# Attention block: transposed probabilities meet the values two slots later, and two instructions get a fixed place in their engines' orders

## Chip, cores and metric

The kernel runs as one program on 1 core of one Trainium2 chip. The metric is device time in microseconds (us) of one execution, the median of several runs. Below, PE is the tensor engine (with PEld its weight loader), DVE the vector engine, ACT the scalar engine, POOL the GpSimd engine and SP the sync engine, which here issues nearly all transfers, in one fixed order.

## What is computed

One hybrid block on a sequence of 1024 tokens and 1024 channels: a convolution branch, an attention branch, a gated sum of both, and a feed-forward part. The change lies in the attention branch. Cut to it, the reference is

```python
for window, dilation in ((128, 1), (512, 4), (2048, 16)):
    o_g, lse_g = dilated_window_attention(q, k, v, slopes, window, dilation)   # blocks of 128, previous and own block as keys
    outs.append(o_g); lses.append(lse_g)
mix = softmax(stack(lses), axis=0)          # per token and head, over the three groups
o = einsum('gbsh,gbshd->bshd', mix, stack(outs))
y_b = o.reshape(B, S, ATTN_DIM) @ w_attn_out
```

There are 16 heads of 64 channels. Matrix products are made at more than one rounded product's accuracy: each operand is split into a rounded part and its remainder (`hi` and `lo`, `ph` and `pl`), and the products of the parts are summed.

## The kernel before

**Slots.** The attention stage is a software pipeline of 128 slots, 8 for each of the 16 heads, followed by 13 more in which it drains (loop at L1114 to L1172). PE, ACT, DVE and POOL run in the order in which this loop is written. SP is not in that list: a scheduler places its transfers, by their dependencies and by when it expects them to be ready. A slot `at` has the place `at % 8` in its head. In order, a slot does the following.

- `score` (L928 to L954): the products of queries and keys for one group of query blocks. Places 0 to 3 score blocks 3, 2, 1, 0 (the head's first half); place 4 scores `far` (queries of the second half against keys of the first, by residue mod 4); places 5, 6 and 7 score blocks 7, 6, and 4 with 5. DVE adds the mask and takes the row minimum (`least`, L928 in the profile), ACT exponentiates (`powers`, L972).
- `fill(FRONT[place])`: filler steps for PE. One step is three 128x512 matmuls of another product (gate logits, then the convolution's output projection, tiles `gate` and `ya`, L120 to L122), whose results are spilled.
- `flip` of the slot 12 earlier (`BACK`): PE transposes up to four 128x128 pieces of probabilities into the PSUM tile `pp` (L1023), ACT rounds it to `ph` (L1044), DVE takes the remainder `pl` (L1045). Places 4, 5 and 6 flip the groups (0), (1), (2,3) of the first half, place 7 nothing, places 0 to 3 the groups far, (4), (5), (6,7,3) of the second.
- `weigh` of the groups that the slot before flipped (list `pend`): PE multiplies `ph` (L1061) and `pl` (L1062) with the values `v` or `vf` into the PSUM tile `o`, one tile for each half head. After a half's last group, `result` (L1065) copies `o` to `ot` on ACT (L1070) and spills it.
- `fill(BEHIND[place])`: more filler steps.

`pp`, `o`, `gate` and `ya` share one pool of four PSUM banks (`psB`); a bank is given to the next tile when its last reader is done.

**Statistics of the second half.** Far and near scores of the same token must be normalised together, though they lie on different partitions. Each side therefore sends its row minimum and sum to the other's layout: `near_to_far` by four small transfers (L989, `other<-own`), `far_out` and `far_to_near` by a write to DRAM and a read of it (L992 `dstat<-own`, L995 `other<-dstat`). `far_out` belongs to place 6, `near_to_far` to place 0 and `far_to_near` to place 1 of the next head. At place 5 DVE compares the two (`compare`, L999), at place 6 `combine` (L1006 to L1008) forms the factors, and POOL scales the probabilities by them (`times`, L975), the far ones first. Then the flips of places 0 to 3 may run.

**Loads.** At place 1 `head(h + 1)` asks for the next head's queries, keys (two transfers `kk`) and mask (`m`, L749); at place 5 `values` asks for `v` and `vf`.

**Before the slots.** The last step of the stage ahead is a product into the PSUM tile `gx` (`product(X, ...)`, L878), which ACT copies away as `c` (L880). The pool of two large PSUM tiles that holds `gx` then holds score tiles.

Of the kernel before, what the change touches and what calls it, by code (L numbers as in the profile page):

```python
# [32 lines left out]

LAG = 2
WARM = 7
FRONT = (0, 2, 0, 1, 0, 1, 1, 0)
BEHIND = (0, 0, 0, 1, 2, 0, 1, 1)
BACK = 12
READ = 5
COPIES = (-1, 0, 1)  # L40
APART = (2, 3, 4, 5, 6)
START = (1, 1, 1, 1, 0, 0, 0, 0, 0, 0, 0, 0)
# [19 lines left out]
def block_kernel(ctx: ExitStack, tc: tile.TileContext, x, xT, x0, g2, pack, mask,  # L62
# [243 lines left out]
    if True:  # L306
# [426 lines left out]
        def conv_result(c):  # L733
# [4 lines left out]
                           scale=pk[:, C_CG + c : C_CG + c + 1])  # L738
            act.dma_start(da[:, c, :], ordered)

        def head(h):
            hp, r, g8 = h // 2, (h % 2) * DH, h // 8
            q = p2.tile([P, T], F32R, tag="q", bufs=2, name=f"q_{h}")
            kk = p2.tile([P, 2, T], F32R, tag="kk", bufs=2, name=f"kk_{h}")
            m = p2.tile([P, 640], F32, tag="m", bufs=2, name=f"m_{h}")
            fetch(q, dq[g8].rearrange("p s c t -> (p s) c t")[2 * r : 2 * r + P, hp % 4, :])
            for s in range(2):
                fetch(kk[s:P:2], dk[g8][r : r + DH, :, hp % 4, :])
            sp.dma_start(m, mask[h])  # L749
            return q, kk[:, 0], kk[:, 1], m  # L750

        cover(COVER)
# [65 lines left out]
        with tc.manual_schedule(engines=hand):  # L818
            for n in range(2):
                xz[n] = gate_first(n, firsts[n])  # L820
                begun(n)
            load(1, 0)
            for n, (a, b) in enumerate(PAIRS):
                X = xz[n][:, 0:512]
                Y = bank_ps(f"gy_{n}")
                (sh, sl), (gh, gl) = pw[n]["s12"], pw[n]["s3"]
                inner = 0 < n < N - 1
                if n + 2 < N:
                    load(n + 2, 0)
                if n == 3:  # L830
                    p1_cm.__exit__(None, None, None)
                    p2_cm = tc.tile_pool(name="ph2", bufs=1, reuse_waits="tile")
                    p2 = p2_cm.__enter__()
                    pool2.append(p2)
                if n + 1 < N:
                    load(n + 1, 1)
                if n == 3:
                    tiles[0] = head(0)
                parts(n, "s4", "s4")
                if n == 0:  # L840
                    fourth()
                if inner:
                    parts(n + 1, 0, "v")
                product(X, sh[:, 4:8], sl[:, 4:8], *form["t2"], False)
                c12 = quarter(f"c12_{n}")
                act.activation(c12, X, AF.Copy)
                product(Y, sh[:, 0:4], sl[:, 0:4], *form["t1"], True)
                p5 = quarter(f"p5_{n}")
                act.activation(p5, Y, AF.Copy)
                if n == N - 1:  # L850
                    act.activation(warm, mhalf[:, 0:7], AF.Exp)
                if n == 0:
                    rs8 = conv_factors()
                if n == 2:
                    for c in (2, 3, 4, 5):
                        conv_result(c)
                product(X, gh[:, 0:4], gl[:, 0:4], *b12, False)
                if n == 1:
                    conv_spread(rs8)
                tt_(p5, X, p5, add)  # L860
                sp.dma_start(dgate[b][:, 512:1024], p5)
                if n + 1 < N:
                    sums(n + 1)
                if inner:
                    xz[n + 1] = big_ps(f"gx_{n + 1}")
                    for i in range(2):
                        product(xz[n + 1][:, i * 512 : i * 512 + 512], *(t[:, 4 * i : 4 * i + 4] for t in pw[n + 1]["v"]),
                                *left[i], True)
                    parts(n + 1, 2, "s12")
                    begun(n + 1)  # L870
                    for c in {1: (0, 1), 2: (6, 7)}.get(n, ()):
                        conv_result(c)
                else:
                    product(Y, *pw[n]["s4"], *b22, False)
                    tt_(c12, Y, c12, add)
                    if n + 1 < N:
                        parts(n + 1, 2, "s12")
                product(X, gh[:, 4:8], gl[:, 4:8], *form["t4"], False)  # L878
                c21 = quarter(f"c21_{n}")
                act.activation(c21, X, AF.Copy)  # L880
                sp.dma_start(dgate[b][:, 0:512], c21)
                if inner:
                    product(Y, *pw[n]["s4"], *b22, False)
                if n + 1 < N:
                    parts(n + 1, 1, "s3")
                if inner:
                    tt_(c12, Y, c12, add)
                sp.dma_start(dgate[a][:, 512:1024], c12)
# [7 lines left out]
    if True:  # L896
# [89 lines left out]

        def near_to_far(h):
            for i in range(4):
                sp.dma_start(other[h][32 * i : 32 * i + 32, 1], own[h][:, 0, i])  # L989

        def far_out(h):
            sp.dma_start(dstat[h % 2], own[h][:, 1])  # L992

        def far_to_near(h):
            sp.dma_start(other[h][:, 0], dstat[h % 2].rearrange("(i a) r s -> (a r) i s", i=4))  # L995

        def compare(h):
            f = ready2("both", [P, 2, 4], F32, 2, f"both_{h}")
# [111 lines left out]
        with tc.manual_schedule(engines={ENG.Activation, ENG.DVE, ENG.PE, ENG.Pool}):  # L1110
            apart = lambda at: at % 8 in APART or not 0 <= at < len(slots)
            pend = []
            fill(1)
            for at in range(len(slots) + BACK + 1):  # L1114
                count[2] += 1
                cur = slots[at] if at < len(slots) else None
                front, behind = (FRONT[at % 8], BEHIND[at % 8] + (START[at] if at < BACK else 0)) if cur else TAIL
                new = []
                if cur is not None:
                    h, half, n = cur  # L1120
                    place = at % 8
                    if place == 4:
                        statistics(h)
                    if place == 5:
                        values(h)
                    if place == 1 and h + 1 < H:
                        tiles[h + 1] = head(h + 1)
                    new = score(h, tiles[h], SCORES[half][n])
                for unit in late:
                    share(*unit)  # L1130
                if len(pieces) > 2 and apart(at):
                    piece_high(2)
                fill(front)
                for n, soon in enumerate(COPIES):
                    if at == 0 and soon < 0 or cur is not None and (at - soon) % 8 == 0 and at - soon < len(slots):
                        by_residue((at - soon) // 8 if at else 0, n)
                flips = []
                if BACK <= at < len(slots) + BACK:
                    fh, fhalf, fn = slots[at - BACK]
                    if FLIPS[fhalf][fn]:  # L1140
                        flips.append(flip(fh, fhalf, FLIPS[fhalf][fn]))
                for w in pend:
                    done = weigh(*w) or done
                pend = flips
                late = []
                if done is not None:
                    result(*done)
                    done = None
                for ago, ready in ((BACK - 2, combine), (BACK - 3, compare)):
                    if 0 <= at - ago < len(slots) and slots[at - ago][1:] == (1, 0):  # L1150
                        ready(slots[at - ago][0])
                for unit in new:
                    powers(*unit)
                if cur is not None and half == 0:
                    late = new
                for ago, n0, send in ((2, 0, far_out), (1, 3, near_to_far), (READ, 0, far_to_near)):
                    if 0 <= at - ago < len(slots) and slots[at - ago][1:] == (1, n0):
                        send(slots[at - ago][0])
                if at == len(slots):
                    p2_cm.__exit__(None, None, None)  # L1160
                    hb2.append(ctx.enter_context(tc.tile_pool(name="hb2a", bufs=1, reuse_waits="tile")))
                    oT = [[hb2[0].tile([P, KT, 512], F32R, tag=f"hb{a}0", name=f"oT{a}0")] for a in range(2)]
                    heads = [o_fetch(0, k) for k in range(0, KT - 2, 2)]
                if at - len(slots) in (4, 5, 8, 9, 10, 11, 12):
                    o_step(heads)
                if at == len(slots) + BACK - 4:
                    heads.append(o_fetch(0, KT - 2))
                if apart(at):
                    piece_low()
                fill(behind)  # L1170
                if apart(at + 1):
                    piece_high(2)  # L1172
            for _ in gates:
# [627 lines left out]
```

## Time and profile before

| What | us |
|---|---|
| median of 3 runs (1698.5 to 1700.75) | 1699.01 |
| the profiled execution's own time | 1695.4 |
| its span, first to last instruction | 1693.6 |
| of the span: slots of the attention stage, about | 570 to 878 |

The profile describes one execution. A row of a group names the line, the engine, the operation, output and inputs, shape and count, then busy time, mean duration of one, and the idle time ahead of it with what ended it. A row of waits names who waited and for what, the total, how many times, and the longest. A row of the timeline has the start, the duration, and in brackets the engine's idle time before it. Matmuls overlap, so the distance between starts, not the duration of one, is what a matmul costs. PE is reported busy for 1681.4 of 1693.6 us.

### The profile page before, as it was taken

How to read it: one execution, taken by the hardware profiler on the slowest of the kernel's cores; microseconds unless marked ns; L12 is line 12 of the kernel's file. 1: busy time of each engine (PE TensorE's matmuls, PEld its weight loads, DVE VectorE, ACT ScalarE, POOL GpSimd, SP SyncE). 2: the span in 40 equal slices, each digit the busy share in tenths (PEclk: the TensorE clock that was granted, in tenths of full speed). 3: DMA queues.
4: the chain of work that ended last, by engine and by line, in shares of the span. 5: the costliest groups of instructions: out<-in, count | busy, mean ns of one | idle time of the engine just before them, and what ended most of it. 6: DMA issues, size and time to landing. Idle time of an engine off the chain costs nothing.

```text
span 1693.6 us, 22622 instructions
## 1 busy us (share of the span) xinstructions
PE 1681.4 (99%) x7939; PEld 1397.1 (82%) x7939; DVE 1303.1 (77%) x2114; ACT 787.9 (47%) x1351; POOL 224.3 (13%) x300
## 2 busy tenths in 40 slices
PE   9999999999999999999999999999999999999999
PEld 7888888888888888888888888888888888888887
DVE  6999999999876567767658654887777677789863
ACT  5411233233245478767646433544544455543431
POOL 0000132033000255555410000000000000000000
PEclk9999999999999999999999999999999999999999
DMA  9411145344555977886769594622222222499851
GB/s 375 153 50 50 50 137 162 125 137 137 175 178 195 320 226 238 261 243 201 221 214 333 187 335 147 227 99 76 75 90 85 87 75 87 145 366 322 287 172 50
DMA packets 187121, 300.24 MB, mean 177 GB/s; under 512 B 32256, under 2 KB 90240, under 8 KB 186496
## 3 DMA queue, kind: packets, MB, share of 16 engines
q1 hardware_dynamic: 185712, 294.48, 52.1%
q10 hardware_dynamic: 1296, 4.33, 0.6%
q8 instruction: 62, 1.02, 0.2%
q14 instruction: 51, 0.42, 0.1%
HBM read 214.74 MB, written 83.95 MB: 176 GB/s over the span
## 4 chain that ended last, share of the span: by engine, by line
PE 92%; DMA 3%; DVE 2%; ACT 1%; issue 1%; SPq 0%; POOL 0%; ACTq 0%; DVEq 0%
PE dx L1607 7%; PE xz L144 6%; PE xz L145 6%; PE xz L146 6%; PE dy L1607 5%; PE qkv L139 5%; PE qkv L137 5%; PE qkv L138 5%; PE y L145 2%; PE y L144 2%; PE y L146 2%; PE pp L1023 2%; PE wo L138 2%; PE wo L139 2%; PE wo L137 2%; PE o L1062 2%
## 5 line engine op out<-in xcount | busy, mean ns | idle before, releaser
L137 PE MATMUL qkv<-hi_qkv,hT 128*128 128x512 f32 x384 | 151.2, 395 | 0.0
L139 PE MATMUL qkv<-hi_qkv,hT 128*128 128x512 f32 x384 | 149.8, 391 | 0.0
L138 PE MATMUL qkv<-lo_qkv,hT 128*128 128x512 f32 x384 | 149.8, 391 | 0.0
L1510 DVE SCALAR_TENSOR_TENSOR u<-u,pk 128x1023 f32<-128x1023 f32 x88 | 112.1, 1275 | 1.2 <-ACT u L1508 0.9
L113 POOL TENSOR_TENSOR rs<-ss,mhalf 128x8 f32<-128x8 f32 x32 | 66.3, 2074 | 294.0 <-DVE ss L112 294.0
L1045 DVE TENSOR_TENSOR pl<-pp,ph 128x512 fp32r<-128x512 f32 (+1 forms) x95 | 58.7, 618 | 46.7 <-ACT ph L1044 46.5
L586 DVE SCALAR_TENSOR_TENSOR cacc<-csum,both,cacc 128x512 f32<-128x512 f32 x120 | 89.4, 745 | 0.3
L586 DVE SCALAR_TENSOR_TENSOR cacc<-apad,pk,cacc 128x512 f32<-128x512 f32 x120 | 88.2, 745 | 0.0
L89 DVE TENSOR_TENSOR lo_uv<-raw_uv,hi_uv 128x1024 fp32r<-128x1024 f32 x20 | 24.5, 1226 | 79.4 <-ACT hi_uv L88 79.4
L139 PEld LDWEIGHTS qkv<-hi_qkv,hT 128*128 128x128 f32 x384 | 72.1, 188 | 15.0
L586 DVE SCALAR_TENSOR_TENSOR codd<-apad,pk,codd 128x513 f32<-128x513 f32 x112 | 83.7, 748 | 0.7 <-ACT codd L579 0.7
L138 PEld LDWEIGHTS qkv<-lo_qkv,hT 128*128 128x128 f32 x384 | 72.2, 188 | 14.3
L137 PEld LDWEIGHTS qkv<-hi_qkv,hT 128*128 128x128 f32 x384 | 72.1, 188 | 14.2
L928 DVE CUSTOM_DVE_ANT_0 p<-s,m 128x512 f32<-128x512 f32 (+1 forms) x120 | 59.1, 502 | 17.2 <-POOL pf L975 6.3
L1044 ACT ACTIVATE ph<-pp 128x512 fp32r<-128x512 f32 (+1 forms) x95 | 51.5, 542 | 43.9 <-PE pp L1023 43.1
L144 PE MATMUL xz<-h2left,hi_uv 128*128 128x512 f32 x176 | 68.6, 390 | 0.0
L144 PE MATMUL xz<-blk_t,hi_s3g 128*128 128x512 f32 x176 | 68.6, 390 | 0.0
L146 PE MATMUL xz<-h2left,lo_uv 128*128 128x512 f32 x176 | 68.5, 389 | 0.0
L145 PE MATMUL xz<-h2left,hi_uv 128*128 128x512 f32 x176 | 68.5, 389 | 0.0
L145 PE MATMUL xz<-blk_t,hi_s3g 128*128 128x512 f32 x176 | 68.5, 389 | 0.0
L146 PE MATMUL xz<-blk_t,lo_s3g 128*128 128x512 f32 x176 | 68.5, 389 | 0.0
L1508 ACT ACTIVATE u<-u,pk 128x1024 f32<-128x1024 f32 x44 | 54.5, 1239 | 9.5 <-DVE u L1497 4.5
(479 smaller groups left out, 5056.5 us busy)
## 6 DMA issues: line engine op xcount, KB each, us to landing
wr<-w_down SPq DMA_DIRECT2D x45, 512.0 KB, 5.9
kk<-dk SPq DMA_DIRECT2D x32, 512.0 KB, 6.1
gr<-dff SPq DMA_DIRECT2D x62, 256.0 KB, 5.4
raw_qkv<-w_qkv SPq DMA_DIRECT2D x24, 512.0 KB, 4.9
dff<-u SPq DMA_DIRECT2D x22, 512.0 KB, 2.6
raw_uv<-w_up SPq DMA_DIRECT2D x21, 512.0 KB, 3.7
raw_ug<-w_up SPq DMA_DIRECT2D x20, 512.0 KB, 3.6
dv<-v SPq DMA_DIRECT2D x16, 512.0 KB, 2.8
```

Of the source, the lines that this page charges most:

```text
L113: pool.tensor_tensor(out=dst, in0=tmp, in1=mhalf[:, : tmp.shape[1]], op=ALU.pow)
L137: pe.matmul(ps, ah, hi[:, k % 2, :], start=(k == 0), stop=False)
L138: pe.matmul(ps, ah, lo[:, k % 2, :], start=False, stop=False)
L139: pe.matmul(ps, al, hi[:, k % 2, :], start=False, stop=(k == KT - 1))
L144: pe.matmul(o, wh[:, k, :], bh[:, k, :], start=(start and k == 0), stop=False, skip_group_check=not start)
L145: pe.matmul(o, wh[:, k, :], bl[:, k, :], start=False, stop=False, skip_group_check=not start)
L146: end = pe.matmul(o, wl[:, k, :], bh[:, k, :], start=False, stop=(k == 3), skip_group_check=not start)
L586: dve.scalar_tensor_tensor(out=out_, in0=src[:, i : i + size], scalar=w(i), in1=out_, op0=ALU.mult, op1=ALU.add)
L928: dve.tensor_tensor_reduce(out=pt, in0=s, in1=m, scale=-1.0, scalar=3e38, op0=ALU.add, op1=ALU.min, accum_out=nm)
L1045: dve.tensor_tensor(out=runs(pl[:, c]), in0=order(pp[:, c]), in1=runs(ph[:, c]).bitcast(F32), op=ALU.subtract)
L1510: dve.scalar_tensor_tensor(out=acc[:, d:], in0=src[:, : T - d], scalar=w(2 - d), in1=acc[:, d:], op0=ALU.mult, op1=ALU.add)
L1607: pe.matmul(banks[n][:, cols], a[:, c], b[:, d], start=(start and i == 0 and m == 0), stop=(stop and i == nf - 1 and m == 2), skip_group_c ...
```

## The change

Groups flipped in one slot are multiplied with the values two slots later (`DEEP`), and one slot later again from the fourth slot of the drain (`NEAR_END`). The filler steps are dealt out anew: 10 for 8 slots as before, now 3 of them ahead of the flip and 7 at the slot's end, where it was 5 and 5. The load of the values moves from place 5 to place 6. The read of the far statistics is tied behind the last transfer noted in `queued`, which is the next head's mask load, or the last `near_to_far` transfer where no head follows. The filler step at the end of slot 0 is tied behind the last matmul of the product ahead of the slots.

```diff
-FRONT = (0, 2, 0, 1, 0, 1, 1, 0)
-BEHIND = (0, 0, 0, 1, 2, 0, 1, 1)
+FRONT = (0, 1, 0, 0, 0, 0, 1, 1)
+BEHIND = (0, 1, 0, 2, 2, 0, 1, 1)
 BACK = 12
 READ = 5
+DEEP = 2
+NEAR_END = 4
+VALUES = 6
...
+        queued = []
+
         def head(h):
...
-            sp.dma_start(m, mask[h])
+            queued[:] = [sp.dma_start(m, mask[h])]
...
-                product(X, gh[:, 4:8], gl[:, 4:8], *form["t4"], False)
+                paired = product(X, gh[:, 4:8], gl[:, 4:8], *form["t4"], False)
...
         def near_to_far(h):
             for i in range(4):
-                sp.dma_start(other[h][32 * i : 32 * i + 32, 1], own[h][:, 0, i])
+                queued[:] = [sp.dma_start(other[h][32 * i : 32 * i + 32, 1], own[h][:, 0, i])]
...
         def far_to_near(h):
-            sp.dma_start(other[h][:, 0], dstat[h % 2].rearrange("(i a) r s -> (a r) i s", i=4))
+            with tc.issue_after(queued[0].ins):
+                sp.dma_start(other[h][:, 0], dstat[h % 2].rearrange("(i a) r s -> (a r) i s", i=4))
...
-                    if place == 5:
+                    if place == VALUES:
                         values(h)
...
-                for w in pend:
-                    done = weigh(*w) or done
-                pend = flips
+                pend.append(flips)
+                while len(pend) > (DEEP if at < len(slots) + NEAR_END else 1):
+                    for w in pend.pop(0):
+                        done = weigh(*w) or done
...
-                fill(behind)
+                with tc.issue_after(paired.ins) if not at else ExitStack():
+                    fill(behind)
```

`tc.issue_after(x)` sets an order of issue on x's engine and no wait for x's end.

The instructions are the same on every engine; PE, ACT and SP run them in another order, DVE with one instruction moved, POOL unchanged. Three places matter. Line numbers of the changed kernel are 3 to 6 higher, and names end in a running number.

PE, places 6 and 7 of head 13's scores, where head 12's first half is weighed (`o_12_0`): the flip of group (2,3), `pp_12_0_2`, and what follows it. Before:

```order
L1023 MATMUL pp_12_0_2_7970<-ident_70,p2_12_7555 128x128
L1023 MATMUL pp_12_0_2_7970<-ident_70,p3_12_7528 128x128 x2
L1061 MATMUL o_12_0_7954<-ph_12_0_1_7947,v_12_7687 128x384
L1062 MATMUL o_12_0_7954<-pl_12_0_1_7948,v_12_7687 128x384
L120 MATMUL ya_5_0_7818<-aT00_5247,hi_co5_7437 128x512
L121 MATMUL ya_5_0_7818<-aT10_5248,hi_co5_7437 128x512
L122 MATMUL ya_5_0_7818<-aT00_5247,lo_co5_7438 128x512
L924 MATMUL s_13_4_8000<-kk_13_7549,q_13_7548 128x256
L925 MATMUL s_13_4_8000<-kk_13_7549,q_13_7548 128x256
L924 MATMUL s_13_4_8000<-kk_13_7549,q_13_7548 128x256
L925 MATMUL s_13_4_8000<-kk_13_7549,q_13_7548 128x256
L1061 MATMUL o_12_0_7954<-ph_12_0_2_7971,v_12_7687 128x256
```

With the change, from the same flip on:

```order
L1029 MATMUL pp_12_0_2_7964<-ident_70,p2_12_7555 128x128
L1029 MATMUL pp_12_0_2_7964<-ident_70,p3_12_7521 128x128 x2
L1067 MATMUL o_12_0_7972<-ph_12_0_0_7903,v_12_7705 128x512
L1068 MATMUL o_12_0_7972<-pl_12_0_0_7904,v_12_7705 128x512
L123 MATMUL ya_5_0_7830<-aT00_5269,hi_co5_7428 128x512
L124 MATMUL ya_5_0_7830<-aT10_5270,hi_co5_7428 128x512
L125 MATMUL ya_5_0_7830<-aT00_5269,lo_co5_7429 128x512
L929 MATMUL s_13_4_7992<-kk_13_7549,q_13_7548 128x256
L930 MATMUL s_13_4_7992<-kk_13_7549,q_13_7548 128x256
L929 MATMUL s_13_4_7992<-kk_13_7549,q_13_7548 128x256
L930 MATMUL s_13_4_7992<-kk_13_7549,q_13_7548 128x256
L123 MATMUL ya_5_0_7830<-aT00_5269,hi_co5_7428 128x512
```

and further on, at place 0 of the next head:

```order
L929 MATMUL s_14_30_8015<-kk_14_7795,q_14_7794 128x512
L930 MATMUL s_14_30_8015<-kk_14_7795,q_14_7794 128x512
L1029 MATMUL pp_12_1_far_8023<-ident_70,pf_12_7645 128x128 x4
L1067 MATMUL o_12_0_7972<-ph_12_0_2_7965,v_12_7705 128x256
L1068 MATMUL o_12_0_7972<-pl_12_0_2_7966,v_12_7705 128x256
```

The group (2,3) is weighed right after place 7's scores before, and behind the next head's first scores and far flip with the change; in its old place stand a filler step and group (1).

SP, the transfers of head 11's statistics (`own_11`, `other_11`) and of head 13's loads. Before:

```order
L992 DMA dstat1_140<-own_11_7392 128x8
L249 DMA dya2_102<-ya_2_1_7432 128x512
L995 DMA other_11_7393<-dstat1_140 128x4x2
L989 DMA other_11_7393<-own_11_7392 32x4x2 x2
L155 DMA q_13_7548<-dq1_75 128x1024
L155 DMA kk_13_7549<-dk1_77 64x2x1024
L1072 DMA do_108<-ot_10_0_7518 128x512
L989 DMA other_11_7393<-own_11_7392 32x4x2 x2
L155 DMA kk_13_7549<-dk1_77 64x2x1024
L749 DMA m_13_7550<-mask 128x640
```

With the change:

```order
L997 DMA dstat1_140<-own_11_7390 128x8
L252 DMA dya2_102<-ya_2_1_7423 128x512
L158 DMA v_11_7460<-dv1_79 128x8x128
L1078 DMA do_108<-ot_9_1_7453 128x512
L994 DMA other_11_7391<-own_11_7390 32x4x2 x2
L158 DMA q_13_7548<-dq1_75 128x1024
L158 DMA kk_13_7549<-dk1_77 64x2x1024
L994 DMA other_11_7391<-own_11_7390 32x4x2 x2
L158 DMA kk_13_7549<-dk1_77 64x2x1024
L754 DMA m_13_7550<-mask 128x640
L1078 DMA do_108<-ot_10_0_7540 128x512
L1001 DMA other_11_7391<-dstat1_140 128x4x2
```

The read of `dstat` stood nearly behind the write that it waits for, and all of the next head's loads behind the read; now it comes last.

PE, the end of the product ahead of the slots and the second score of head 0 (`s_0_31`). Before, with one filler step some 40 rows earlier, between the first score and this product:

```order
L144 MATMUL gx_4_4554<-gt40_3354,hi_s3_4_4614 128x512
L145 MATMUL gx_4_4554<-gt41_3355,hi_s3_4_4614 128x512
L146 MATMUL gx_4_4554<-gt40_3354,lo_s3_4_4615 128x512
L924 MATMUL s_0_31_4741<-kk_0_4493,q_0_4492 128x384
L925 MATMUL s_0_31_4741<-kk_0_4493,q_0_4492 128x384
```

With the change:

```order
L149 MATMUL gx_4_4554<-gt40_3354,lo_s3_4_4615 128x512
L123 MATMUL gate_12_0_4736<-hT00_229,hi_gt12_4722 128x512
L124 MATMUL gate_12_0_4736<-hT10_230,hi_gt12_4722 128x512
L125 MATMUL gate_12_0_4736<-hT00_229,lo_gt12_4723 128x512
L929 MATMUL s_0_31_4741<-kk_0_4493,q_0_4492 128x384
L930 MATMUL s_0_31_4741<-kk_0_4493,q_0_4492 128x384
```

The filler step now stands between the product and the score.

## The prediction

> **What bounds the kernel now.** First the page's busy times, then the attention stage alone in the view by windows.
>
> ```profile
> span 1693.6 us, 22622 instructions
> PE 1681.4 (99%) x7939; PEld 1397.1 (82%) x7939; DVE 1303.1 (77%) x2114; ACT 787.9 (47%) x1351; POOL 224.3 (13%) x300
> 600.00:880.00 280.00, 273.32 (x1613) 232.19 (x1612) 194.18 (x647) 201.68 (x562) 133.69 (x226) 1.00 0.74 225
> ```
>
> PE sets the time: 12.2 us of the span are idle, and 6.7 of these lie in the 280 us of the attention stage, at a granted clock of 1.00. DVE (194 of 280), ACT and POOL have room, so only waits can be won. The waits of that stretch say whose:
>
> ```profile
> PEld o L1062 <- DVE pl L1045: 7.3, 9, 1.9
> PE o L1062 <- DVE pl L1045: 5.3, 7, 1.7
> DVE both L999 <- DMA kk<-dk: 4.4, 4, 2.0
> PEld pp L1023 <- POOL p L975: 4.3, 14, 0.3
> PEld pp_far L1023 <- POOL pf L975: 1.6, 8, 0.2
> PEld s L924 <- issue: 1.6, 2, 1.0
> PE s L924 <- DMA kk<-dk: 0.5, 1, 0.5
> PEld o L1062 <- DVE pl_far L1045: 0.5, 1, 0.5
> ```
>
> Most of it is the second product of a weighing, which waits until DVE has made the remainder `pl`. To see what the waits cost in time, including what hides in matmuls that overlap, I measure heads by the starts of their far scores in PE's timeline:
>
> ```profile
> 612.62 0.63 PE L963 MATMUL s_far<-far_k,far_q 128*128 128x256 f32 x4
> 629.24 0.64 PE L963 MATMUL s_far<-far_k,far_q 128*128 128x256 f32 x4
> 839.06 0.63 PE L963 MATMUL s_far<-far_k,far_q 128*128 128x256 f32 x4
> ```
>
> A head without a marked wait takes 629.24 - 612.62 = 16.62 us. The 13 heads from 612.62 to 839.06 take 226.44, where 13 x 16.62 = 216.06: 10.4 us are lost, and that is the stake here. [...]
>
> The longest wait shows the mechanism, in the timelines of PE and DVE:
>
> ```profile
> 809.42 0.49 PE L1023 MATMUL pp<-ident,p 128*128 128x128 f32 x3
> 811.26 0.28 PE L1061 MATMUL o<-ph,v 128*128 128x256 f32 x1
> 813.26 0.39 PE L1062 MATMUL o<-pl,v 128*128 128x256 f32 x1 [1.71 <-DVE pl L1045]
> ...
> 808.69 0.56 DVE L1045 TENSOR_TENSOR pl<-pp,ph 128x384 fp32r<-128x384 f32 x1 [0.80 <-ACT ph L1044]
> 811.29 0.17 DVE L999 TENSOR_TENSOR both<-own,other 128x8 f32<-128x8 f32 x1 [2.04 <-DMA kk<-dk]
> 812.65 0.55 DVE L1045 TENSOR_TENSOR pl<-pp,ph 128x384 fp32r<-128x384 f32 x1
> ```
>
> The group flipped at 809.42 is weighed at 811.26, 1.8 us later, but DVE stood 2.04 us at the compare of statistics (L999 waits for `other`; the row names the transfer that landed last), and its queue holds the remainder behind that. Why the statistics are late, SP's timeline and the transfers show:
>
> ```profile
> 795.74 0.38 SPq L992 DMA_DIRECT2D dstat<-own  x1
> 801.39 0.37 SPq L995 DMA_DIRECT2D other<-dstat  x1
> 801.85 1.26 SPq L989 DMA_DIRECT2D other<-own  x2
> 805.12 1.57 SPq L989 DMA_DIRECT2D other<-own  x2
> 807.42 0.59 SPq L749 DMA_DIRECT2D m<-mask  x1
> ...
> SPq L995 <- DMA dstat<-own: 68.7, 15, 5.4
> ...
> m<-mask SPq DMA_DIRECT2D x13, 320.0 KB, 6.3
> other<-own SPq DMA_DIRECT2D x60, 1.0 KB, 3.7
> dstat<-own SPq DMA_DIRECT2D x15, 4.0 KB, 5.7
> other<-dstat SPq DMA_DIRECT2D x15, 4.0 KB, 1.9
> ...
> 796.09 0.49 ACT L972 ACTIVATE p<-p,own 128x256 f32<-128x256 f32 x1
> ```
>
> SP stands 5.3 us from the write of `dstat` to its landing (4.6 on average), and everything behind waits with it: the near statistics, queries, keys, mask.
>
> **The change part by part.**
>
> *Two slots instead of one.* A slot is 16.62 / 8 = 2.1 us on average, so the 1.8 us of cover above become about 4, more than the longest wait of 1.9 asks. At stake are 7.3 + 0.5 of the loader's waits, less the one at the very end, which lies in the drain, where weighing again follows by one slot:
>
> ```profile
> 875.36 0.44 PE L1062 MATMUL o<-pl,v 128*128 128x384 f32 x1 [1.11 <-DVE pl L1045]
> ...
> 794.78 0.60 ACT L1070 ACTIVATE ot<-o 128x512 f32<-128x512 f32 x1 [0.38 <-PE o L1062]
> ```
>
> That leaves 7.8 - 1.1 = 6.7. Not all of it goes, because a flip's bank is freed by the same remainder: in the built program group (6,7,3) is transposed into the bank of group (4), two slots on, and in eight heads the first half's `o` takes the bank of the `o` just finished, with only a score, a filler step and three transposes (about 1.3 us) between, for ACT's copy of 0.60. That copy now stands behind the rounding of the flip before, so some 0.4 us are spare where ACT was idle before it. Bounds: nothing comes back, or half (3.3). I take 1.0 back, nearer to nothing, as ACT's copy was waiting for PE and not the reverse. Gain 5.7.
>
> *Filler steps moved.* The same ten steps a head, so no work is added. A step (three matmuls 0.23 apart, 0.7 us) that stood ahead of the flip of group 1 now lies ahead of group (1)'s weighing at place 7. The far flip at place 0 comes no sooner after `combine`, so its 1.6 us of waiting for POOL shrink; bounds 0 and 1.6, taken 1.0. The 4.3 us of the loader for POOL at `pp` are 0.3 a head, of which the starts show about 0.1, inside the 16.62; bounds 0 and -1.4, taken 0.
>
> *The read of far statistics last.* SP no longer stands ahead of the loads. It is free once ACT has finished the exponentials of blocks 4 and 5, at 796.09 + 0.49 and 0.1 more for the sum, some 4.7 us before 801.39. Keys come earlier by as much: the two waits of a score for keys (PE 0.5 and loader 1.6, of which at least 0.5 is time lost) mostly go; taken 1.0. The near statistics come 3 to 4 us earlier. The far ones now come last: from 801.85 to the mask's end at 808.01 is 6.2 us of issue, so the read goes out at 796.7 + 6.2 = 802.9, and behind the loads it must be expected to take the mask's 6.3 us and not the 1.9 that it took on a drained queue. It lands at 809.2; DVE was ready at 811.29 - 2.04 = 809.25. So it is just in time in the worst head. Since place 5 holds a filler step less, DVE will be ready up to half a microsecond sooner: I add 0.5 us over all heads, between 0 and the slower rival below. (The Trainium skill, "DMA: Bandwidth & Descriptors", section "Two DMAs through the same engine are not ordered", states that descriptors of one queue on one DMA engine start in order. It speaks against this edit, for the small read then starts after the mask's descriptors; 6.3 against 1.9 agrees. By the 1.9 the read would land at 804.8, with room to spare.)
>
> *The first filler step.* At the stage's beginning the second score waits for ACT to copy `gx`:
>
> ```profile
> 579.24 0.39 PE L146 MATMUL gx<-gt,lo_s 128*128 128x512 f32 x1
> 579.66 0.60 ACT L880 ACTIVATE c<-gx 128x512 f32<-128x512 f32 x1 [7.85 <-PE gx L146]
> 580.31 0.44 PE L924 MATMUL s<-kk,q 128*128 128x384 f32 x1 [0.69 <-ACT c L880]
> ```
>
> With a step of 0.7 us behind the product instead of ahead of it, the copy is hidden: gain 0.7, bounds 0 and 0.8 (580.31 - 579.24 less 0.23).
>
> *The values one slot later* are loaded a slot later and used a slot later: nothing.
>
> Sum: -5.7 - 1.0 - 1.0 - 0.7 + 0.5 = -7.9 us, so the profiled execution of 1695.4 would become 1687.5. The median of 1699.0 stands 3.6 above that execution; I carry the difference over: 1691.1.
>
> **The rivals.**
>
> *Everything goes* (0.15): the 10.4 of the heads, 0.7 at the start, and part of the 0.1 a head at `pp`: about -12, 1687. For it, every wait now has a slot more; against it, the banks.
>
> *The wait moves down the chain* (0.17). PE no longer stands at the weighing, runs on, and meets the far flip before POOL has scaled it. The 7.41 us of POOL's own wait in that head end with DVE's factors:
>
> ```profile
> 813.81 1.42 POOL L975 TENSOR_SCALAR pf<-pf,both 128x128 f32<-128x128 f32 x4 [7.41 <-DVE both L1008]
> ```
>
> If the statistics stay as late as now, the heads whose DVE stood (4.4 us) lose it at the flip instead: -7.9 + 4.4 = -3.5, 1695.5. Against it, the near statistics land earlier.
>
> *The banks take it back* (0.11): half of the 6.7 returns and the far flip gains nothing: -7.9 + 2.3 + 1.0 = -4.6, 1694.4.
>
> *Slower* (0.08): the read of far statistics lands late in every head. Its place is the compare, which holds all that DVE does next, then POOL's scaling (3.5 us, from 813.81 above to 817.30, where its next cast begins), then the far flip. Two slots do not cover that, for the flip itself is late. The mask's landing varies:
>
> ```profile
> DMA to landing us min/median/max: 5.7/6.3/9.7
> ...
> 817.30 1.13 POOL L921 CAST far_q<-q 128x512 fp32r<-128x512 f32 x1
> ```
>
> Each 0.1 us beyond the 6.3 costs 13 x 0.1 = 1.3 us, so it decides from 6.3 + 7.9 / 13 = 6.9 us on; at 7.2 us it is 13 x 0.9 = 11.7 - 7.9 = +3.8, 1702.8. For it, the loads are now issued without a pause; against it, their bytes are the same.
>
> *The change does nothing* (0.04), as the stake is made up by other waits: 1699.
>
> **How the numbers follow.** My forecast has 0.45, its own range 1688 to 1695. Two versions of this kernel can be told apart from about 0.2% (3.4 us): faster is below 1695.6, slower above 1702.4. Faster: 0.44 of my forecast, 0.15, about half of the chain (0.07) and of the banks (0.06): 0.72. Slower: 0.07, most of that rival. Same: 0.21. Range 1686.5 to 1699.5: below it lies a part of "everything goes", above it the slower rival and some of no effect.
>
> **What would show it.** Right: the waits of PE and its loader for `pl` fall from 7.8 us to below 2.5, with the drain's left; heads take 16.6 to 16.9 us and not 17.4 on average; SP's wait for `dstat` is gone; DVE stands at the compare for less than 6 us in all; the gap at 580 is gone. Wrong: new waits of `o` for ACT's copy or of `pp` for `pl` (banks), longer waits of `pp_far` for POOL (chain), or the read of `dstat` that takes over 7 us to land and a compare that waits in most heads (slower).

## The result, and the profile after

The changed kernel takes 1685.66 us (median of 6 runs, 1684.90 to 1686.58) beside 1697.34 us of the kernel before (6 runs, 1693.84 to 1700.75): a ratio of 0.9932, interval 0.9918 to 0.9946. It is faster, by 11.7 us between the medians. The forecast was 1691.1 us with a range from 1686.5: right in sign, but the time lies 0.8 us below the range. The profiled execution of the changed kernel took 1686.58 us, so between the two profiled executions the gain is 8.8 us, where the sum of the forecast was 7.9.

Page and view by windows of the changed kernel:

```profile
span 1684.8 us, 22651 instructions
PE 1676.5 (100%) x7939; PEld 1398.5 (83%) x7939; DVE 1303.8 (77%) x2114; ACT 785.0 (47%) x1351; POOL 223.9 (13%) x300
600.00:880.00 280.00, 276.51 (x1648) 238.94 (x1647) 198.08 (x647) 200.80 (x565) 133.18 (x226) 1.00 0.78 234
```

PE idles 8.3 us of the span (12.2 before) and 3.5 in the attention stage (6.7 before). The busy share shows little of this; the heads show it, in PE's timeline:

```profile
612.65 0.64 PE L968 MATMUL s_far<-far_k,far_q 128*128 128x256 f32 x4
...
814.05 0.64 PE L968 MATMUL s_far<-far_k,far_q 128*128 128x256 f32 x4
830.41 0.64 PE L968 MATMUL s_far<-far_k,far_q 128*128 128x256 f32 x4
```

The first of these starts where it did before (612.62); the last comes 8.65 us earlier. The 13 heads take 217.76 us, not 226.44. The last head here takes 16.36, and others 16.35: less than the 16.62 that the prediction took for a head free of waits.

The waits of the same stretch in the changed kernel:

```profile
PE pp L1029 <- DVE pl L1051: 1.3, 2, 1.0
PE o L1068 <- DVE pl L1051: 1.1, 1, 1.1
PE o L1067 <- ACT ot L1076: 0.4, 1, 0.4
...
PEld pp L1029 <- POOL p L980: 3.0, 11, 0.3
PEld pp L1029 <- DVE pl L1051: 2.7, 4, 1.4
PEld o L1068 <- DVE pl L1051: 1.6, 2, 1.3
...
PEld pp_far L1029 <- POOL pf L980: 0.2, 1, 0.2
...
DVE both L1005 <- DMA other<-dstat: 1.5, 1, 1.5
...
SPq L997 <- ACT pf L977: 46.3, 14, 5.2
```

The wait of weighing for `pl` is down to the one in the drain (5.3 before on PE). Waits of `pp` for `pl` are new: these are the banks. DVE stands at the compare once, for 1.5 us, and SP's long wait for `dstat` has become a wait ahead of the write, for ACT's exponentials, where only later transfers are behind it. The transfers themselves:

```profile
m<-mask SPq DMA_DIRECT2D x13, 320.0 KB, 6.3
other<-own SPq DMA_DIRECT2D x60, 1.0 KB, 4.8
other<-dstat SPq DMA_DIRECT2D x15, 4.0 KB, 6.0
dstat<-own SPq DMA_DIRECT2D x14, 4.0 KB, 1.6
```

The read of `dstat` takes 6.0 us behind the mask, where it took 1.9; the forecast was 6.3. Of the gap ahead of the second score nothing is left, as PE's timeline has it:

```profile
579.42 0.39 PE L125 MATMUL gate<-hT,lo_gt 128*128 128x512 f32 x1
579.82 0.45 PE L929 MATMUL s<-kk,q 128*128 128x384 f32 x1
```

### The profile page after: what moved, and what is told of

Its sections match the earlier page's. It is cut to its first block, busy times and chain, and to the rows that moved or that the text cites. A ratio compares the mean times of both kernels' runs of the same rounds, so it can differ in the third digit from the quotient of the medians.

```text
span 1684.8 us, 22651 instructions
## 1 busy us (share of the span) xinstructions
PE 1676.5 (100%) x7939; PEld 1398.5 (83%) x7939; DVE 1303.8 (77%) x2114; ACT 785.0 (47%) x1351; POOL 223.9 (13%) x300
## 4 chain that ended last, share of the span: by engine, by line
PE 91%; DMA 2%; issue 2%; DVE 1%; POOL 1%; ACT 1%; SPq 0%; POOLq 0%; DVEq 0%; ACTq 0%
PE dx L1615 7%; PE xz L147 6%; PE xz L148 6%; PE xz L149 6%; PE dy L1615 5%; PE qkv L142 5%; PE qkv L140 5%; PE qkv L141 5%; PE y L147 2%; PE y L149 2%; PE y L148 2%; PE wo L140 2%; PE wo L141 2%; PE wo L142 2%; PE pp L1029 2%
```

## The experiments

Times in us. "Ratio" is to the kernel before, run on the same chip in between; its interval is of 95%. "Heads" is the time of the 13 heads in the profiled execution, from the third start of `s_far` to the sixteenth.

| Kernel | Median (lowest to highest, runs) | Ratio (interval) | Heads |
|---|---|---|---|
| before again (e1) | 1697.32 (1693.30 to 1700.26, 11) | 1.0004 (0.9995 to 1.0013) | 227.20 |
| tie of the read alone (e2) | 1690.66 (1689.86 to 1691.26, 6) | 0.9969 (0.9958 to 0.9980) | 220.75 |
| depth, steps, values, no ties (e3) | 1686.67 (1684.90 to 1687.73, 5) | 0.9944 (0.9933 to 0.9956) | 217.59 |
| tie of the first step alone (e4) | 1697.26 (1693.61 to 1699.05, 12) | 1.0002 (0.9993 to 1.0011) | 229.55 |
| new filler steps alone (e5) | 1694.46 (1693.40 to 1695.44, 10) | 0.9986 (0.9977 to 0.9995) | 224.72 |
| change with old filler steps (e6) | 1686.42 (1685.91 to 1687.38, 4) | 0.9940 (0.9926 to 0.9953) | 217.77 |
| change, deep to the end (e7) | 1689.20 (1688.76 to 1690.11, 5) | 0.9957 (0.9943 to 0.9970) | 217.70 |
| change, read far too late (e8) | 1774.61 (1774.22 to 1775.19, 4) | 1.0459 (1.0445 to 1.0473) | 299.63 |
| depth with the read first (e9) | 1687.36 (1686.59 to 1690.45, 5) | 0.9950 (0.9938 to 0.9963) | 217.05 |
| change, one addition later (e10) | 1686.48 (1685.12 to 1686.79, 5) | 0.9940 (0.9926 to 0.9953) | 217.45 |
| the change again (e11) | 1685.62 (1685.10 to 1686.15, 5) | 0.9937 (0.9925 to 0.9950) | 217.44 |

### e1: the kernel before, again

No edit. The three times of the kernel before that the prediction had lay 3.6 us above its profiled execution.

> The kernel before, unchanged, for a second profile of it. Theory 1 (its waits hang on when transfers land, so they differ from execution to execution): the two profiles of this kernel differ in the 13 heads of the attention stage (226.4 us in the first), by 1 to 4 us, and the rest of the span agrees within 1 us. Theory 2 (chips or sessions differ as a whole): the heads agree within 1 us and the difference of 3.5 us between the first three and the later three times shows in other stages as well.

Over all batches the kernel before ran 65 times, from 1693.30 to 1700.75 us with the median at 1696.43; the changed kernel ran 11 times, within 1684.90 to 1686.58. The two profiles differ less than the first theory has it: by 0.8 us in the 13 heads and 0.3 outside them. With the profile of e4 (below; it differs from this kernel by one tie) the place of the scatter shows. The three spans are 1693.6, 1694.7 and 1697.1 us, their 13 heads take 226.44, 227.20 and 229.55, and the rest 1467.2, 1467.5 and 1467.6. So what these executions differ by is made in the attention stage; none near 1700 us was profiled. Up to 570 us the view by windows has PE busy for 568.68 us here and 568.87 in the first profile, but in PE's timeline of this execution the heads are uneven:

```profile
698.29 0.63 PE L963 MATMUL s_far<-far_k,far_q 128*128 128x256 f32 x4
719.11 0.63 PE L963 MATMUL s_far<-far_k,far_q 128*128 128x256 f32 x4
737.33 0.63 PE L963 MATMUL s_far<-far_k,far_q 128*128 128x256 f32 x4
```

One head takes 20.82 us and the next 18.22; the first profile had none above 18.9. Inside the long one DVE stood 2.79 us at the compare and PE at the weighing behind it:

```profile
708.93 0.48 PE L1062 MATMUL o<-pl,v 128*128 128x256 f32 x1 [1.91 <-DVE pl L1045]
...
710.06 0.63 PE L121 MATMUL ya<-aT,hi_co 128*128 128x512 f32 x1
710.49 0.63 PE L122 MATMUL ya<-aT,lo_co 128*128 128x512 f32 x1
```

That is 1.91 us, 0.2 more than the longest in the first profile, but then the filler matmuls start 0.43 us apart instead of 0.23. The windows (the column after POOL is the granted clock) say why:

```profile
707.00:708.00 1.00, 0.02 (x1) 0.00 (x0) 0.45 (x3) 0.08 (x1) 0.00 (x0) 1.00 0.92 335
708.00:709.00 1.00, 0.07 (x1) 0.07 (x1) 0.96 (x5) 0.70 (x3) 0.00 (x0) 1.00 1.01 308
709.00:710.00 1.00, 1.00 (x4) 0.97 (x5) 0.96 (x6) 0.38 (x3) 0.52 (x2) 0.53 0.99 349
710.00:711.00 1.00, 1.00 (x4) 0.74 (x3) 0.08 (x2) 1.00 (x4) 1.00 (x4) 0.50 0.99 355
711.00:712.00 1.00, 1.00 (x5) 0.70 (x4) 0.00 (x0) 0.34 (x2) 1.00 (x2) 0.50 1.15 356
712.00:713.00 1.00, 1.00 (x7) 1.00 (x6) 0.70 (x2) 0.18 (x1) 1.00 (x4) 0.76 1.13 385
```

The granted clock fell to half for the 3 us after the wait: 0.47 + 0.50 + 0.50 + 0.24 = 1.7 us of work lost on top of the wait. So in these profiles the waits that the change removes are also what makes the kernel before scatter, and a little more wait in one execution costs twice.

### e2: the tie of the read alone

Against the kernel before (and `queued` filled as in the change):

```diff
         def far_to_near(h):
-            sp.dma_start(other[h][:, 0], dstat[h % 2].rearrange("(i a) r s -> (a r) i s", i=4))
+            with tc.issue_after(queued[0].ins):
+                sp.dma_start(other[h][:, 0], dstat[h % 2].rearrange("(i a) r s -> (a r) i s", i=4))
```

> Only the read of far statistics tied behind the mask load; weighing one slot later and the filler steps as before. Theory 1 (the depth of two slots carries most of the gain): -1 to -3 us against before, the two-microsecond wait at the compare gone, but PE's loader still waits 4 us or more for the remainder. Theory 2 (late statistics caused the waits): -5 us or more, the loader's waits for the remainder below 3 us.

Alone it brings 5.7 us (1690.66 against 1696.37 of its batch), half of the whole change. Its waits:

```profile
PEld o L1065 <- DVE pl L1048: 5.0, 6, 1.7
PE o L1065 <- DVE pl L1048: 3.7, 5, 1.4
DVE both L1002 <- DMA raw_a<-da: 0.7, 1, 0.7
```

DVE's compare waits 0.7 us instead of 6.0 (4.4 for `kk` and two of 0.8 for others in the first profile), the waits for `pl` that hung on it shrink, and the runs lie within 1.4 us. The gain is what the second theory expected; the loader's waits of 5.0 us that stay are what the first did.

### e3: depth without the ties

Against the changed kernel both ties are taken out; `DEEP`, `NEAR_END`, `VALUES` and the new `FRONT` and `BEHIND` stay.

```diff
-            with tc.issue_after(queued[0].ins):
-                sp.dma_start(other[h][:, 0], dstat[h % 2].rearrange("(i a) r s -> (a r) i s", i=4))
+            sp.dma_start(other[h][:, 0], dstat[h % 2].rearrange("(i a) r s -> (a r) i s", i=4))
...
-                with tc.issue_after(paired.ins) if not at else ExitStack():
-                    fill(behind)
+                fill(behind)
```

> Two slots between flip and weighing, with the values at place 6 and the filler steps dealt out anew; neither of the two ties. Theory 1 (the depth carries most): -5 to -8 us, and the head without a wait falls from 16.6 to 16.35 us. Theory 2 (late statistics): -2 to -4 us, since the wait moves to the far flip, which then waits for POOL by over 4 us in all.

It brings 9.7 us, nearly all of the change and more than either theory expected. 9.7 and e2's 5.7 make 15.4, more than the whole: the two edits mend the same waits. But the scheduler also used the freedom to put the load of `v` and a spill of `ot` between the write of `dstat` and its read, so that SP waited only 10.6 us for it here (68.7 before), and DVE stands at the compare for 1.4 us in all, not 6.0. So the statistics come earlier here too, without the tie. That left open how much was the depth itself; e9 answers it in part.

### e4: the tie of the first step alone

Against the kernel before:

```diff
-                fill(behind)
+                with tc.issue_after(paired.ins) if not at else ExitStack():
+                    fill(behind)
```

> Only the filler step of slot 0 tied behind the product ahead of the slots. Both theories: -0.5 to -0.8 us, the gap of 0.69 us ahead of the second score gone; if the 0.3 us that heads 0 and 1 lost with the whole change come from this edit, they lose them here too and the gain is near 0.

The gap of 0.69 us is gone (the second score follows its filler step at 579.53 without a wait), and the first `s_far` starts at 585.29, not 586.08. The median doesn't show it: by the interval the effect lies between -1.2 and +1.9 us, and 0.7 is below what this comparison can tell. Heads 0 and 1 take 10.34 and 16.06 us here (10.33 and 16.21 before), so what they lose with the whole change doesn't come from this tie: head 0 takes 10.54 to 10.57 us in every kernel with the new filler steps and 10.32 to 10.34 in every one with the old.

### e5: the new filler steps alone

Against the kernel before:

```diff
-FRONT = (0, 2, 0, 1, 0, 1, 1, 0)
-BEHIND = (0, 0, 0, 1, 2, 0, 1, 1)
+FRONT = (0, 1, 0, 0, 0, 0, 1, 1)
+BEHIND = (0, 1, 0, 2, 2, 0, 1, 1)
```

> Only the filler steps dealt out anew; weighing one slot later, no ties. Theory 1 (the lower floor of a head, 16.35 against 16.62 us, comes from the order of small and large matmuls that the new steps and the new depth make together, and from the wait for POOL ahead of the flip of group 4): the floor stays between 16.45 and 16.65 us, and the waits for the remainder grow beyond 10 us, since steps that covered them are gone: slower than before by 2 us or more. Theory 2 (the new steps by themselves make the floor): the quickest heads take 16.35 us.

2.1 us faster, with an interval of 0.9977 to 0.9995, where the first theory expected 2 us slower. The longest waits for `pl` shrink, but the shortest of the 13 heads got longer, 16.74 us, which neither theory has, and the loader's waits for POOL with it:

```profile
PEld pp L1023 <- POOL p L975: 9.1, 23, 0.8
PEld o L1062 <- DVE pl L1045: 6.6, 17, 1.5
```

With fewer filler steps ahead of the flip, PE reaches group (4) sooner than POOL has scaled it. So the new dealing does not shorten the head by itself. Where the 2.1 us come from is not worked out.

### e6: the change with the old filler steps

Against the changed kernel, the two lines of e5 the other way.

> The whole change but with the filler steps where they were before. Theory 1: floor between 16.45 and 16.65 us, waits for the remainder below 4 us, about 2 to 4 us slower than the whole change. Theory 2 (depth and ties make the floor): the quickest heads take 16.35 us and the time is within 1.5 us of the whole change.

PE's timeline:

```profile
612.56 0.63 PE L968 MATMUL s_far<-far_k,far_q 128*128 128x256 f32 x4
...
830.33 0.63 PE L968 MATMUL s_far<-far_k,far_q 128*128 128x256 f32 x4
```

The heads take 217.77 us, as in the changed kernel, with the shortest at 16.35 to 16.38, as the second theory has it. What the steps move is the loader's wait for POOL: 3.3 us at the far flip and 0.3 at `pp` here, 0.2 and 3.0 in the changed kernel. The shorter head comes from the depth: among the 13 heads, the shortest is at 16.58 or more in every kernel here without it, and at 16.35 or so in every one with it, e8 apart. The medians (1686.42 here, 1685.66 and 1685.62 for the changed kernel in other batches) differ by 0.8 us, which is too little to tell apart.

### e9: depth with the read ahead of the loads

Against e3: `READ = 3` and `VALUES = 5`, and the transfers that SP issued behind the read before are tied behind it again.

```diff
         def near_to_far(h):
-            for i in range(4):
+            with tc.issue_after(read_far[0].ins):
+                for i in range(4):
...
-                        tiles[h + 1] = head(h + 1)
+                        with tc.issue_after(read_far[0].ins) if read_far else ExitStack():
+                            tiles[h + 1] = head(h + 1)
```

> Two slots and the new filler steps, without the two ties, but now with the read of the far statistics ordered ahead of the near ones and of the next head's queries, keys and mask, and the values asked for at place 5 again, so that SP stands at the read as in the kernel before. Theory 1, depth alone is enough: SP's wait for dstat comes back (40 us or more over 15 heads, where depth alone without this order had 10.6), DVE stands at the compare again for 3 us or more in all, but the waits of o for pl stay under 4 us with the drain's and the 13 heads take 217 to 219 us; median 1685.5 to 1688. Theory 2, much of the gain of depth alone came from the order of SP that it brought along: heads 220 to 223 us, the wait sits at the far flip (pp_far for POOL, over 3 us) or at the scores; median 1689 to 1693.

Time and heads are those of the first theory, its conditions are not. From the waits of SP, PE and DVE in this kernel:

```profile
SPq L1001 <- DMA dstat<-own: 31.8, 14, 7.2
...
PE s L929 <- DMA kk<-dk: 1.1, 1, 1.1
PE o L1068 <- DVE pl L1051: 0.9, 1, 0.9
...
DVE both L1005 <- DMA other<-own: 0.4, 1, 0.4
```

SP stands 31.8 us at the read (less than the 40 expected, since a load of `v` often fills the gap), a wait for keys of 1.1 us is back, and the heads take 217.05 us all the same. So the depth brings its gain without the read's place behind the loads. But DVE stands at the compare for 0.4 us, where 3 or more were expected: the late statistics did not come back, so that two slots would cover them is not shown. One of the five runs here took 1690.45, more than any of the 11 of the changed kernel; whether its order of SP makes it steadier, one run does not tell.

### e7: two slots to the end of the drain

```diff
-NEAR_END = 4
+NEAR_END = 11
```

> The whole change with two slots kept up to the eleventh slot of the drain and not the fourth. Theory 1: the last wait for the remainder (1.1 us idle) goes, -1 us against the whole change, as far as the last results are not spilled later. Rival: the last results come a slot later and the next stage's first product waits for them, 0 or +1 us.

3.5 us slower than the changed kernel (1685.66, in another batch), which neither theory expected: there the drain waits 1.09 us for `pl`, here 3.04. DVE's and PE's timelines of this kernel:

```profile
866.68 1.22 DVE L1104 TENSOR_TENSOR raw_o<-raw_o,oT 128x1024 f32<-128x1024 f32 x1 [3.24 <-DMA oT<-do]
867.82 0.55 DVE L1051 TENSOR_TENSOR pl<-pp,ph 128x384 fp32r<-128x384 f32 x1
...
868.42 0.65 PE L1068 MATMUL o<-pl,v 128*128 128x384 f32 x1 [3.04 <-DVE pl L1051]
```

Weighing later makes `ot` and its spill later; the transfer that reads the spill back lands later, DVE stands at the addition that needs it (3.24 us, 1.00 in the changed kernel), and the remainder `pl` is queued behind that addition. The view by windows shows the rest of the price, the clock again:

```profile
865.09:868.50 3.41, 0.37 (x3) 0.08 (x1) 1.82 (x3) 0.56 (x1) 0.00 (x0) 1.00 1.03 414
868.50:871.91 3.41, 3.41 (x10) 2.83 (x11) 3.40 (x4) 2.87 (x4) 0.00 (x0) 0.50 0.37 118
```

1.95 us more of waiting and half of 3.41 us, 1.7, for the clock make 3.7, and 3.5 was measured.

### e8: the read far too late

To price the slower rival, the read of the far statistics is issued from `compare`, tied behind the preceding head's last spill:

```diff
         def compare(h):
+            far_to_near(h)
...
-                for ago, n0, send in ((2, 0, far_out), (1, 3, near_to_far), (READ, 0, far_to_near)):
+                for ago, n0, send in ((2, 0, far_out), (1, 3, near_to_far)):
...
-            sp.dma_start(do_[h // 2].rearrange("i (d r) t -> (i d) r t", r=2)[:, h % 2, cs], tmp)
+            queued[:] = [sp.dma_start(do_[h // 2].rearrange("i (d r) t -> (i d) r t", r=2)[:, h % 2, cs], tmp)]
```

> The whole change, but the read of far statistics is issued only behind the spill of the preceding head's second half, at place 5, where the compare wants it. Theory 1 (statistics run through compare, factors, POOL and far flip, and two slots at the weighing do not cover that): the compare waits 2 us or more in most heads, the heads take 1 to 4 us more each, the time rises by 15 us or more over the whole change, and PE's loader waits for POOL ahead of the flips. Rival (depth covers it): the compare waits as long, but the time rises by less than 5 us.

89 us slower than the changed kernel. Its waits:

```profile
DVE both L1006 <- DMA other<-own: 37.0, 7, 5.9
DVE both L1006 <- DMA other<-dstat: 27.8, 5, 7.3
PE s L929 <- DVE own L933: 36.7, 13, 5.2
PE pp_far L1030 <- POOL pf L980: 11.9, 14, 3.5
```

and the window over its heads:

```profile
600.00:920.00 320.00, 274.58 (x1436) 227.26 (x1434) 167.81 (x609) 186.33 (x530) 125.58 (x210) 0.88 0.61 177
```

DVE stands at the compare for 5 to 7 us in nearly every head, as the slower rival of the prediction had it, but PE waits mostly not at the far flip: it waits at the next scores, whose PSUM tile DVE has still to read. A head takes 6.3 us more than in the changed kernel, beyond the 1 to 4 that the first theory gave. PE's two waits are 48.6 us. The clock, 0.88 over 320 us, is worth up to another 38: less, as part of the low clock falls into waits, where it costs nothing. The two make up most of the 89 us; an exact sum is not worked out.

### e10 and e11: one addition later, and the change again

In e10 the addition that holds `pl` in the drain is done a slot later:

```diff
-                if at - len(slots) in (4, 5, 8, 9, 10, 11, 12):
+                if at - len(slots) in (4, 5, 8, 10, 11, 12):
```

> The whole change, and in the drain one step of the addition of head outputs (add of raw_o and oT on DVE, which waited 1.00 us for its transfer in the changed kernel) a slot later, behind the remainder pl of group (5). Theory 1, the drain's wait of 1.1 us hangs on that transfer: the waits of o for pl in the drain go, and the median falls by 0.8 to 1.2 us, to about 1684.7; nothing else moves. Theory 2, DVE has so much to do there that the wait comes back at another place (the add is late for what follows, or the mixture gg): median within 0.5 us of the changed kernel, 1685.2 to 1686.2.

> The changed kernel itself once more, as the yardstick of the run above: all theories expect 1685 to 1686.6, and a scatter below 2 us, where the kernel before scatters by 7.

The wait for `pl` in the drain does go. Another takes its place, as the second theory has it, the next product waiting for its weights, in PE's timeline of e10:

```profile
867.98 0.50 PE L123 MATMUL yb<-oT,hi_ao 128*128 128x512 f32 x1 [0.67 <-ACT hi_ao L91]
```

e10 is not faster than the change measured beside it (1686.48 against 1685.62). No kernel tried here beats the changed one.

## Why the prediction was right in sign and too high

**The bound and what held it: right.** PE was held by late remainders, these by DVE's stand at the compare, and that by the statistics: e2, which only brings the statistics earlier, gains 5.7 us. That a longer cover does the rest is not shown. e3 and e9 gain 9.7 and 8.4 us without the tie, but in them too the statistics are hardly late: DVE stands at the compare for 1.4 and 0.4 us.

**"I carry the difference over": the step that failed.** The forecast for the profiled execution was 1687.5, and 1686.58 came. To it the prediction added 3.6 us, by which the median of three runs stood above the profiled one. Of 65 runs the median is 1696.43, only 1.0 above that execution; the three runs shown all lay in the upper part of that range. More than that, the step was wrong in kind: as far as the profiles show, the scatter of before comes from the very waits that the change removes (e1), so a difference made by them should not have been carried over. In the changed kernel the profiled execution lies 0.9 above its median. The miss of 5.4 us is thus 3.6 carried, 0.9 by which the sum fell short (8.8 against 7.9), and 0.9 by which the median lies below the profiled execution. Without the 3.6 the forecast would have been 1687.5, and its range, moved by as much, 1682.9 to 1695.9 with the measured time inside.

**"A head without a marked wait takes 16.62 us": wrong as a floor.** With depth it takes 16.35 (e3, e6), so the stake was 226.44 - 13 x 16.35 = 13.9 us and not 10.4. The prediction put the loader's 4.3 us at `pp` for POOL at 0 and called its 0.1 a head part of the floor. In a clean head of e2 the second transpose at `pp` (778.55) starts 0.23 us behind the first and so 0.13 late; in the clean heads of e6 and of the change none does, and the loader has no wait for POOL at `pp` there. A further 0.1 is spread over the 100 matmuls, whose order is another. With depth the first half's last weighing stands between the far flip and the flip of group (4), which gives POOL that time; this last is read from the order and not tested by itself.

**Two slots, -6.7 and +1.0 at the banks.** The waits of weighing for `pl` went as said, with the drain's left. The banks returned 1.7 us of idle time (`pp` for `pl` 1.3, `o` for ACT's copy 0.4), 1.0 of it in one head; 1.0 was assumed, within its bounds. The heads say what the depth adds beside the tie. Beyond 13 clean heads of their own kernel, the heads lose 10.4 us before, 5.1 in e2 (220.75 - 13 x 16.59) and 5.2 with the whole change. So where the statistics are early by the tie, the depth takes nothing off the waits: the 2.3 us that PE still waits for `pl` in the heads of e2 go, and the banks' 1.7 come. What it adds is the shorter clean head, 13 x 0.24 = 3.1 us, which the prediction had at 0. Without the tie the depth comes to the same (5.0 in e3), with the statistics earlier as well. Of the 5.2 us that the change leaves, 4.2 lie in five heads that follow each other, 645.93 to 731.92, in which DVE is busiest (78% of the time, 72% in the heads around); the banks' waits of 1.0 and 0.4 and most of the loader's waits for POOL at `pp` are among them, and which engine makes these heads long is not worked out.

**The read last: the sizes missed both ways.** The landing (6.0 for 6.3) and the few waits at the compare (1.5 us for an allowance of 0.5 lost) were right. But its worth was put at 0.5 net beside depth's 5.7, when alone it is worth 5.7 itself. The prediction costed it as the removal of the waits for keys and left out that it also makes the statistics early enough. In the sum this did not hurt, since depth had been credited with the same waits: that is luck. And 6.3 against 1.9 could not show the order of transfers, as the one was the mask's and the other the read's own; the read's 6.0 behind the mask fits it.

**Filler steps, -1.0; first step, -0.7; values, 0.** With the old steps the change is within 0.8 us (e6), so in it the steps are worth about what their term said or less. The far flip's wait does shrink, but the wait for POOL moves on to `pp`. The first step removes its gap, but heads 0 and 1 take 10.55 and 16.51 us in the changed kernel for 10.33 and 16.21, so nothing of it is left at 612.65; head 0's part of that comes with the new filler steps (e4). The later values cost nothing that the waits show.

**The rivals.** "Everything goes" was nearest, though its 1687 had the carried 3.6 in it as well. The chain did not come about: `pp_far` waits 0.2 us for POOL. The slower rival's mechanism is real (e8), but with the read at the mask's end it is not reached.

## What to carry to other kernels

When a kernel scatters more than its successor could, ask which waits make the scatter, and do not carry a difference between runs through an edit that removes them. Two edits that mend the same waits (here the depth and the place of the read) do not add up: cost each alone, and expect little more than the larger. Take the floor of a loop from the kernel's work and not from its best iteration, since small waits that occur in all iterations hide in that.

## What the hardware showed that was not expected

A wait of PE of 1.91 us (e1), 1.85 and 2.98 (e4) or 3.04 (e7) was followed by a granted clock of 0.50 for 3.41 us, some 1.7 us of lost work, while the wait of 1.71 in the first profile of the kernel before passed at 1.00. A single wait does not decide it: in e8 one of 1.54 us (at 901.06) with one of 0.72 behind it was followed by half the clock. In every trace here the clock changes at distances that are whole multiples of 3.41 us (a low clock lasts 3.41 in e1, e4 and e7, and 3.41 to 10.24 in e8), and what divides the cases is PE's idle time within one such stretch. The kernel before, then e4:

```profile
809.77:813.18 3.41, 1.77 (x12) 1.44 (x10) 1.85 (x7) 1.11 (x3) 0.00 (x0) 1.00 0.96 283
813.18:816.59 3.41, 3.33 (x18) 2.77 (x19) 2.11 (x11) 3.13 (x10) 2.78 (x7) 1.00 1.10 357
...
876.10:879.51 3.41, 1.56 (x8) 1.13 (x8) 3.03 (x4) 1.78 (x3) 0.00 (x0) 1.00 0.71 288
879.51:882.92 3.41, 3.41 (x13) 2.93 (x12) 3.41 (x4) 2.25 (x3) 0.00 (x0) 0.50 0.68 183
```

An idle time of 3.41 - 1.77 = 1.64 us in the stretch passed, one of 3.41 - 1.56 = 1.85 did not. In the thirteen traces, every stretch at full clock with more than 1.8 us of idle time was followed by half the clock, and none with 1.64 or less was. Nothing between was met, so the bound lies there, near half of the stretch.

The Trainium skill, "TensorE: Matmul & The Clock Gate", section "HAM oscillation — how this bites in real kernels", has the clock fall for idle gaps above some 3.4 us; here waits of 1.85 and 1.91 us sufficed. The half clock agrees with the table in the section "What's actually happening" of the same page of the Trainium skill, as does a return to full speed after some 3.4 us of work.

A small read issued behind large loads took about their time: the 4 KB of `dstat` landed after 1.9 us when SP had stood still ahead of it, and after 6.0 behind the mask's 320 KB, which took 6.3.
